# Moving three 8 KB buffers and one odd one by 32 bytes: the stationary operands of the down products at the same address modulo 256 as the moving ones

## The chip, the cores and the metric

The kernel runs on one core of a Trainium2 chip. The metric is the device time of one execution in microseconds (us), the median of the runs shown. Five engines work side by side: TensorE (PE in the profile, with its weight loads as PEld) multiplies, VectorE (DVE) and ScalarE (ACT) do elementwise work, GpSimd (POOL) a little, and SyncE (SP) issues the DMAs that bring the weights from HBM. A matmul has two operands in SBUF: the *stationary* one, which a weight load (LDWEIGHTS) puts into the array, and the *moving* one, whose columns are then streamed through it. SBUF addresses below are bytes within a partition.

## What is computed

One decoder layer on 256 tokens of width 2048, float32 throughout:

```python
x = layer_norm(alpha * x + 0.5 * swiglu(x, ffn1_w_gate, ffn1_w_up, ffn1_w_down), ln1_g, ln1_b)
p = x @ w_in                                   # 2048 x 6432
o_attn = diff_attn_group(p[..., :3072], ...)   # 8 heads, causal, ALiBi, two softmaxes subtracted
o_rwkv = rwkv7_group(p[..., 3072:], ...)       # 16 heads of 64, delta-rule state
x = layer_norm(alpha * x + concatenate([o_attn, o_rwkv], -1) @ w_out, ln2_g, ln2_b)
x = layer_norm(alpha * x + 0.5 * swiglu(x, ffn2_w_gate, ffn2_w_up, ffn2_w_down), ln3_g, ln3_b)

def swiglu(x, w_gate, w_up, w_down):           # D_FF = 5632
    return (jax.nn.silu(x @ w_gate) * (x @ w_up)) @ w_down
```

The nine products with the big weight matrices (gate, up and down of two FFNs, the input projection, the output projection) hold nearly all the arithmetic.

## The kernel before

**Dense products.** Every float32 factor is split into a high part in the fp32r format and the low rest, also fp32r, and a product is three matmuls: high times high (line 105), high activations times low weights (line 106), low activations times high weights (line 107). The activations, transposed so that the contraction lies along the partitions, are stationary (128 x 128); a row block of weights, 128 x 512, is moving. `Stream.block` walks a column block of 512 output columns in steps of two row blocks: one 512 KB DMA into `raw`, `wh` = the cast by ScalarE (line 128), `wl` = the rest by VectorE (line 129), then six matmuls for each of the two token tiles `tt` (tokens 0 to 127 and 128 to 255). Token tile 1 follows token tile 0 by up to four steps (`LAG`), so that the matmuls of the two stand mixed in the program.

**FFN.** The 11 column blocks `j` of 512 hidden columns come in two halves, of 6 and 5. For each `j` the gate and up products run with the transposed input `xh`/`xl` as stationary tiles; then `up_done` multiplies them, transposes the result `h` on TensorE (line 221) and splits it into the high and low tiles `hh` (lines 229 and 230). When a half is done, the four column blocks of the down product run over its hidden columns, with `hh` stationary: 24 row blocks in the first half, 20 in the second. They are called the *down stages* here; there are four, 2112 matmuls in all on 704 pairs of tiles.

**Where the tiles lie.** SBUF is nearly full, and the `hh` tiles live in buffers of the pool `hp` that the mixer between the FFNs uses for other things. Blocks `j` = 0 to 2 have 8,192-byte buffers for both token tiles (tags `J0` to `J2`); blocks 3 to 5 have one 4,096-byte buffer per token tile (`H0` to `H2` for token tile 0, `H3` to `H5` for token tile 1). `H3` is also the mixer's `praw`, 4 x 257 floats, which makes it 4,112 bytes long. A buffer's address follows from the order in which the tags are first used, each rounded up to 32 bytes:

```
buffer  FFN use (tt = token tile)   before: address, mod 256   after: address, mod 256
J0      j = 0, both tt              21536   32                 25664   64
J1      j = 1, both tt              29728   32                 33856   64
J2      j = 2, both tt              37920   32                 42048   64
H0      j = 3, tt 0                 46112   32                 50240   64
H3      j = 3, tt 1                 50208   32                 21536 + 32 = 21568   64
H1      j = 4, tt 0                 54336   64                 54336   64
H4      j = 4, tt 1                 58432   64                 58432   64
H2      j = 5, tt 0                 62528   64                 62528   64
H5      j = 5, tt 1                 66624   64                 66624   64
xh, xl  16 tiles of 2048 bytes      70720 ...  64              the same
wh, wl  7 buffers of 4096 bytes each   115776 ...  64          the same
```

Within a buffer the tiles that a matmul takes lie 512, 2048 or 4096 bytes apart, so each has its buffer's residue. In the kernel before, the odd length of `H3` is what moves the residue from 32 to 64 for all that come after it.

**The order of work** is set by the program's scheduler, which emits one instruction stream per engine with semaphore waits. The mixer's small matmuls run as background generators between the steps of the input projection.

The mixer's uses of the buffers that move are `AR` (J0), `SV` (J1), `qq` (J2), `lw` and `TT` (H0); `praw`, an output tile and `yt` stay in `H3` at residue 32.

Of the kernel before, what the change touches and what calls it, by code (L numbers as in the profile page):

```python
# [10 lines left out]
F32 = mybir.dt.float32  # L11
F32R = mybir.dt.float32r
# [4 lines left out]
P = 128  # L17
D = 2048
S = 256
DFF = 5632  # L20
NB = 512
# [16 lines left out]
def build(tc, A, out):  # L38
# [3 lines left out]
    hp = ctx.enter_context(tc.tile_pool(name="hp", bufs=1))  # L42
# [2 lines left out]
    sp = ctx.enter_context(tc.tile_pool(name="sp", bufs=2))  # L45
    dp = ctx.enter_context(tc.tile_pool(name="dp", bufs=1, space=bass.MemoryType.DRAM))
    pa = ctx.enter_context(tc.tile_pool(name="pa", bufs=3, space=bass.MemoryType.PSUM))

    HT = {"lw": "H0", "T1": "H1", "T2": "H2", "k": "H4"}
    uid = [0]  # L50

    def nm(s):
        uid[0] += 1
        return f"{s}_{uid[0]}"
# [119 lines left out]
    def ln_tail(tt, y, st, gt, bt, last):  # L174
        mv = sp.tile([P, 2], F32, tag="mv", name=nm("mv"))
        V.bn_aggr(out=mv, in_=st)
        ve = sp.tile([P, 1], F32, tag="ve", name=nm("ve"))
        V.tensor_scalar(out=ve, in0=mv[:, 1:2], scalar1=LN_EPS, scalar2=None, op0=ALU.add)
        rs = sp.tile([P, 1], F32, tag="rs", name=nm("rs"))
        G.tensor_tensor(out=rs, in0=ve, in1=neghalf, op=ALU.pow)  # L180
        for q in range(4):
            c = slice(q * NB, (q + 1) * NB)
            yq = y[q]
            V.scalar_tensor_tensor(out=yq, in0=yq, scalar=mv[:, 0:1], in1=gt[:, c], op0=ALU.subtract, op1=ALU.mult)  # L184
            V.scalar_tensor_tensor(out=yq, in0=yq, scalar=rs, in1=bt[:, c], op0=ALU.mult, op1=ALU.add)  # L185
            if last:
                nc.sync.dma_start(out=out[tt * P:(tt + 1) * P, c], in_=yq)
            else:
                transpose_split(yq, tt, q, xT)
                nc.scalar.dma_start(out=xs[tt][:, c], in_=yq)  # L190

    def load_gb(pool, g, b, tg, tb, after=None):
        gt = (hp if tg == "J0" else pool).tile([P, D], F32, tag=tg, name=nm("lng"))
        bt = pool.tile([P, D], F32, tag=tb, name=nm("lnb"))
        if after is not None:
            G.tensor_copy(out=gt[:, 0:1], in_=after)
            G.tensor_copy(out=bt[:, 0:1], in_=after)
        nc.gpsimd.dma_start(out=gt, in_=g.to_broadcast([P, D]))
        nc.gpsimd.dma_start(out=bt, in_=b.to_broadcast([P, D]))
        return gt, bt  # L200

    def ffn(fp, wg, wu, wd, lg, lb, res, last, extra=None):
        y = [fp.tile([P, D], F32, tag=f"y{t}", name=nm("y")) for t in range(2)]
        st = [sp.tile([P, 4, 6], F32, tag=f"st{t}", name=nm("st"), bufs=1) for t in range(2)]
        gb = []
        j0 = 0
        for half, nj in enumerate((6, 5)):
            hT = {}
            sg = {}

            def gate_done(tt, acc):
                s = fp.tile([P, NB], F32, tag="sg", name=nm("sg"), bufs=2)
                SC.activation(out=s, in_=acc, func=AF.Silu)  # L213
                sg[tt] = s

            def up_done(tt, acc, j):
                h = fp.tile([P, NB], F32, tag="h", name=nm("h"), bufs=2)
                V.scalar_tensor_tensor(out=h, in0=sg[tt], scalar=0.5, in1=acc, op0=ALU.mult, op1=ALU.mult)  # L218
                tr = tr_bank[-1]()
                for i in range(4):  # L220
                    T.transpose(tr[:, i, :], h[:, i * P:(i + 1) * P], ident)  # L221
                if j < 3:
                    if tt == 0:
                        hT[j] = hp.tile([P, 4, 4, P], F32R, tag=f"J{j}", name=nm("hh"))
                    hi, lo = hT[j][:, 2 * tt], hT[j][:, 2 * tt + 1]
                else:
                    hl = hp.tile([P, 2, 4, P], F32R, tag=f"H{3 * tt + j - 3}", name=nm("hh"))
                    hi, lo = hl[:, 0], hl[:, 1]
                SC.copy(out=hi, in_=tr)  # L229
                V.tensor_tensor(out=lo, in0=tr, in1=hi.bitcast(F32), op=ALU.subtract)  # L230
                hT[(tt, j)] = (hi, lo)

            for j in range(nj):
                c0 = (j0 + j) * NB
                stream.block(wg, c0, NB, KX, x_lhs, gate_done)
                stream.block(wu, c0, NB, KX, x_lhs, lambda tt, acc, j=j: up_done(tt, acc, j))

            def h_lhs(tt, k, hT=hT):
                hi, lo = hT[(tt, k // 4)]
                return hi[:, k % 4, :], lo[:, k % 4, :]  # L240

            if half == 0 and extra is not None:
                extra(hT[(0, 0)][0][:, 0, 0:1].bitcast(F32))
            if half == 1:
                gb = load_gb(fp, lg, lb, "lng", "lnb", hT[(0, 0)][0][:, 0, 0:1].bitcast(F32))

            def down_done(tt, acc, n, half=half, hT=hT):
                c = slice(n * NB, (n + 1) * NB)
                if half == 0:
                    rc = fp.tile([P, NB], F32, tag="rc", name=nm("rc"), bufs=2)  # L250
                    G.tensor_copy(out=rc[:, 0:1], in_=hT[(0, 0)][0][:, 0, 0:1].bitcast(F32))
                    nc.scalar.dma_start(out=rc, in_=res[tt][:, c])
                    V.scalar_tensor_tensor(out=y[tt][:, c], in0=rc, scalar=ALPHA, in1=acc, op0=ALU.mult, op1=ALU.add)
                else:
                    V.tensor_tensor(out=y[tt][:, c], in0=y[tt][:, c], in1=acc, op=ALU.add)
                    V.bn_stats(out=st[tt][:, n, :], in_=y[tt][:, c])
                    if n == 3:
                        ln_tail(tt, [y[tt][:, i * NB:(i + 1) * NB] for i in range(4)], st[tt], gb[0], gb[1], last)

            for n in range(4):  # L260
                ks = [(j0 * 4 + k, k) for k in range(nj * 4)]
                stream.block(wd, n * NB, NB, ks, h_lhs, lambda tt, acc, n=n, f=down_done: f(tt, acc, n))
            j0 += nj
# [686 lines left out]
```

## Time and profile before

| | |
|---|---|
| runs | 2022.15, 2024.24, 2021.31 us; median 2022.15 us |
| profiled execution | 2021.85 us; span of its instructions 2020.1 us |
| PE busy | 1976.9 us (98%), 9671 matmul records |
| DVE, ACT busy | 1149.0 us (57%), 887.6 us (44%) |
| DMA | 373.35 MB, 185 GB/s on average |
| mean granted TensorE clock | 0.989 |
| first FFN, first half | gate and up to 283.4 us, down stage from there to 406.1 us |
| first FFN, second half | gate and up alone from 417.2 to 627.4 us, down stage alone from 639.2 to 745.4 us |
| mixer, output projection, and gate and up of the second FFN's first half | 746.9 to 1534.2 us |
| second FFN, its two down stages | 1546.0 to 1668.6 us and 1901.8 to 2007.9 us |

Between two stages the matmuls of both stand mixed for about 11 us.

The profile's page gives busy times by engine, the span in 40 slices, and groups of instructions by source line with the tiles that they write and read; windows give the same for a stretch of time. A matmul record's duration includes the time that its data needs through the array, so the records of neighbouring matmuls overlap; the distance from one start to the next is the time that one matmul costs. In a timeline view a row is one instruction or, with "x2", a few merged ones, with its start in microseconds from the span's start.

### The profile page before, as it was taken

To read this page: it belongs to the slowest core of one execution; us is meant where nothing else is said; L and a number is where in the kernel's file an instruction comes from. 1 tells how busy PE (TensorE), PEld (TensorE's weight loads), DVE (VectorE), ACT (ScalarE), POOL (GpSimd) and SP (SyncE) were. 2 spreads that over 40 slices of the span, in tenths; PEclk is the share of its full clock that TensorE was granted. 3 is DMA by queue.
4 is the path that set the end of the run, shared out by engine and by line. 5 is a ranking of instruction groups with operands and counts; after the bars stand their busy time and mean duration, and the time that the engine had idled before them with its cause. 6 is when DMAs were issued, how large, how long until landed. Compare 5 with 4: busy or idle time off the path is not lost. (4 is left out here: it accounts for less than half of the span.)

```text
span 2020.1 us, 24928 instructions
## 1 busy us (share of the span) xinstructions
PE 1976.9 (98%) x9671; PEld 1614.6 (80%) x9671; DVE 1149.0 (57%) x1420; ACT 887.6 (44%) x1100; POOL 33.9 (2%) x68
## 2 busy tenths in 40 slices
PE   9999999999999999999999988999999999999997
PEld 7888888888888878888777777788888888888886
DVE  5555544445554566776677866755554444555455
ACT  5444433344444337645574444444443334444432
POOL 0200000000000000000000000000000000000000
PEclk9999999999999999999999979999999999999999
DMA  7766666667666556556435624666666666766553
GB/s 248 214 188 195 186 190 202 205 192 229 193 187 189 188 171 194 177 160 178 139 86 177 198 84 148 210 198 188 196 185 190 203 204 191 230 193 187 189 188 125
DMA packets 202008, 373.35 MB, mean 185 GB/s; under 512 B 22826, under 2 KB 24944, under 8 KB 201120
## 3 DMA queue, kind: packets, MB, share of 16 engines
q1 hardware_dynamic: 182928, 350.53, 58.0%
q10 hardware_dynamic: 17440, 14.29, 2.4%
q0 software_dynamic: 1520, 6.93, 1.0%
q8 instruction: 76, 1.25, 0.3%
q14 instruction: 44, 0.36, 0.1%
HBM read 364.10 MB, written 7.60 MB: 184 GB/s over the span
## 5 line engine op out<-in xcount | busy, mean ns | idle before, releaser
L129 DVE TENSOR_TENSOR wl<-raw,wh 128x1024 fp32r<-128x1024 f32 (+1 forms) x665 | 808.2, 1216 | 662.4 <-ACT wh L128 661.3
L128 ACT CAST wh<-raw 128x1024 fp32r<-128x1024 f32 (+1 forms) x665 | 695.2, 1046 | 851.9 <-PE acc L107 736.8
L107 PE MATMUL acc<-wh,xl 128*128 128x512 f32 (+1 forms) x1952 | 740.7, 391 | 1.6 <-DVE xl L79 1.6
L106 PE MATMUL acc<-wl,xh 128*128 128x512 f32 (+1 forms) x1952 | 736.7, 392 | 1.0 <-DVE wl L129 1.0
L105 PE MATMUL acc<-wh,xh 128*128 128x512 f32 (+1 forms) x1952 | 725.5, 392 | 9.0 <-ACT xh L78 7.6
L105 PEld LDWEIGHTS acc<-wh,xh 128*128 128x128 f32 x1952 | 367.9, 189 | 88.7 <-ACT xh L78 9.3
L106 PEld LDWEIGHTS acc<-wl,xh 128*128 128x128 f32 x1952 | 368.1, 189 | 77.5 <-issue 2.0
L107 PEld LDWEIGHTS acc<-wh,xl 128*128 128x128 f32 x1952 | 367.8, 188 | 76.3 <-DVE xl L79 2.0
L107 PE MATMUL acc<-wh,hh 128*128 128x512 f32 x704 | 258.0, 395 | 0.0
L106 PE MATMUL acc<-wl,hh 128*128 128x512 f32 x704 | 256.7, 394 | 0.0
L105 PE MATMUL acc<-wh,hh 128*128 128x512 f32 x704 | 256.0, 394 | 0.0
L106 PEld LDWEIGHTS acc<-wl,hh 128*128 128x128 f32 x704 | 132.0, 187 | 31.4
L107 PEld LDWEIGHTS acc<-wh,hh 128*128 128x128 f32 x704 | 132.0, 188 | 31.2
L105 PEld LDWEIGHTS acc<-wh,hh 128*128 128x128 f32 x704 | 132.0, 188 | 30.9
L230 DVE TENSOR_TENSOR hh<-tr,hh 128x512 fp32r<-128x512 f32 x44 | 30.4, 691 | 64.4 <-ACT hh L229 64.4
L229 ACT CAST hh<-tr 128x512 fp32r<-128x512 f32 x44 | 25.8, 586 | 91.7 <-PE tr L221 91.6
L218 DVE SCALAR_TENSOR_TENSOR h<-sg,acc 128x512 f32<-128x512 f32 x44 | 30.3, 688 | 35.6 <-PE acc L107 35.6
L213 ACT ACTIVATE sg<-acc 128x512 f32<-128x512 f32 x44 | 26.4, 600 | 43.8 <-PE acc L107 43.7
L577 DVE TENSOR_TENSOR itmp<-U,Y 64x31 f32<-64x31 f32 (+15 forms) x62 | 20.6, 332 | 11.5 <-DMA U<-dU 10.2
L221 PEld LDWEIGHTS tr<-ident,h 128*128 128x128 f32 x176 | 21.8, 139 | 5.7
L221 PE MATMUL tr<-ident,h 128*128 128x128 f32 x176 | 26.3, 272 | 0.0
L579 DVE TENSOR_TENSOR Y<-Y,itmp 64x31 f32<-64x31 f32 (+15 forms) x62 | 20.6, 332 | 1.4
(247 smaller groups left out, 750.2 us busy)
## 6 DMA issues: line engine op xcount, KB each, us to landing
raw<-in_ffn_w_up_dram SPq DMA_DIRECT2D x176, 512.0 KB, 3.9
raw<-in_ffn_w_down_dram SPq DMA_DIRECT2D x176, 512.0 KB, 4.1
raw<-in_ffn_w_gate_dram SPq DMA_DIRECT2D x175, 512.0 KB, 3.9
raw<-in_w_in_dram SPq DMA_DIRECT2D x96, 512.0 KB, 3.9
raw<-in_w_out_dram SPq DMA_DIRECT2D x32, 512.0 KB, 4.6
rc<-xs ACTq DMA_DIRECT2D x16, 256.0 KB, 4.0
lng<-in_ln_g_dram POOLq DMA_DIRECT2D x3, 1024.0 KB, 7.0
lnb<-in_ln_b_dram POOLq DMA_DIRECT2D x3, 1024.0 KB, 9.3
```

The lines of the kernel that those rows point to most:

```text
L105: T.matmul(a, hi, wh[:, j, :w], start=(ki + j == 0), stop=False)
L106: T.matmul(a, hi, wl[:, j, :w], start=False, stop=False)
L107: T.matmul(a, lo, wh[:, j, :w], start=False, stop=(ki + j == last))
L128: SC.copy(out=wh[:, c, :w], in_=raw[:, c, :w])
L129: V.tensor_tensor(out=wl[:, c, :w], in0=raw[:, c, :w], in1=wh[:, c, :w].bitcast(F32), op=ALU.subtract)
L213: SC.activation(out=s, in_=acc, func=AF.Silu)
L218: V.scalar_tensor_tensor(out=h, in0=sg[tt], scalar=0.5, in1=acc, op0=ALU.mult, op1=ALU.mult)
L221: T.transpose(tr[:, i, :], h[:, i * P:(i + 1) * P], ident)
L229: SC.copy(out=hi, in_=tr)
L230: V.tensor_tensor(out=lo, in0=tr, in1=hi.bitcast(F32), op=ALU.subtract)
L577: V.tensor_tensor(out=tv, in0=U[:, 0:j, j:j + 1].to_broadcast([64, j, 32 - j]), in1=Y[:, j:j + 1, j:32].to_broadcast([64, j, 32 - j]), op= ...
L579: V.tensor_tensor(out=Y[:, 0:j, j:32], in0=Y[:, 0:j, j:32], in1=tv, op=ALU.add)
```

## The change

Two edits. `H3` gets its first use before every other tag of its pool, by a tile that nothing reads or writes, of 4 x 258 floats = 4,128 bytes; so it lies first, at 21536, and the other buffers of the pool follow it at 25664 and on, all at residue 64. And the FFN's use of `H3` starts 8 floats, 32 bytes, into the buffer, at 21568, which is residue 64 too; the tiles of `H0`, `H1`, `H2`, `H4` and `H5` are written in the same flat form without the offset. After it, every stationary and every moving tile of all the dense products lies at 64 modulo 256.

```diff
@@ -45,6 +45,8 @@
     dp = ctx.enter_context(tc.tile_pool(name="dp", bufs=1, space=bass.MemoryType.DRAM))
     pa = ctx.enter_context(tc.tile_pool(name="pa", bufs=3, space=bass.MemoryType.PSUM))
+
+    hp.tile([P, 4 * (S + 2)], F32, tag="H3", name="h3")
 
     HT = {"lw": "H0", "T1": "H1", "T2": "H2", "k": "H4"}
@@ -224,8 +226,10 @@
                     hi, lo = hT[j][:, 2 * tt], hT[j][:, 2 * tt + 1]
                 else:
-                    hl = hp.tile([P, 2, 4, P], F32R, tag=f"H{3 * tt + j - 3}", name=nm("hh"))
-                    hi, lo = hl[:, 0], hl[:, 1]
+                    n = 3 * tt + j - 3
+                    o = 8 if n == 3 else 0
+                    hl = hp.tile([P, o + 8 * P], F32R, tag=f"H{n}", name=nm("hh"))
+                    hi, lo = [hl[:, o + c:o + c + NB].rearrange("p (a b) -> p a b", a=4) for c in (0, NB)]
                 SC.copy(out=hi, in_=tr)
                 V.tensor_tensor(out=lo, in0=tr, in1=hi.bitcast(F32), op=ALU.subtract)
```

No instruction is added, removed or moved: on every engine the two programs have the same instructions in the same order, with the same semaphore waits; only addresses differ.

## The prediction

> **What bounds the kernel now.** The page first: busy time by engine, the slices of the span, the groups that prepare the weights, and two windows, the first down stage and the gate and up products that follow it. (A window's columns: its length, then busy time and instructions of PE, PEld, DVE, ACT and POOL, the granted clock, DMA share, GB/s.)
>
> ```profile
> PE 1976.9 (98%) x9671; PEld 1614.6 (80%) x9671; DVE 1149.0 (57%) x1420; ACT 887.6 (44%) x1100; POOL 33.9 (2%) x68
> PE   9999999999999999999999988999999999999997
> PEclk9999999999999999999999979999999999999999
> ```
>
> ```profile
> L129 DVE TENSOR_TENSOR wl<-raw,wh 128x1024 fp32r<-128x1024 f32 x655 | 800.8, 1224 | 659.3 <-ACT wh L128 658.1
> L128 ACT CAST wh<-raw 128x1024 fp32r<-128x1024 f32 x655 | 688.6, 1052 | 836.7 <-PE acc L107 728.2 <-DMA raw<-in_w_in_dram 44.0 <-DMA raw<-in_ffn_w_gate_dram 22.8
> ```
>
> ```profile
> 283.00:406.00 123.00, 123.00 (x534) 99.56 (x533) 59.48 (x53) 46.71 (x45) 1.10 (x6) 1.00 0.65 200
> 417.00:628.00 211.00, 211.00 (x948) 174.72 (x947) 104.95 (x94) 89.22 (x95) 1.36 (x4) 1.00 0.68 200
> ```
>
> TensorE has work in every slice of the FFNs, at the full granted clock. Inside the two windows it is busy all the time, VectorE about half and ScalarE 38 to 42%, and ScalarE's cast mostly waits for matmuls to free a weight buffer, not the other way round. So the FFN's time is the number of matmuls times the distance between two starts, and anything that changes that distance goes to the end one for one.
>
> Next that distance itself. The first view is a timeline inside a down stage (start, duration, instruction); I matched the 7,968 `acc` records of the trace one by one with the program's matmuls to know which `hh` tile each takes.
>
> ```profile
> 303.36 0.39 PE L105 MATMUL acc<-wh,hh 128*128 128x512 f32 x1
> 303.59 0.39 PE L106 MATMUL acc<-wl,hh 128*128 128x512 f32 x1
> 303.82 0.39 PE L107 MATMUL acc<-wh,hh 128*128 128x512 f32 x1
> 304.04 0.39 PE L105 MATMUL acc<-wh,hh 128*128 128x512 f32 x1
> 304.27 0.39 PE L106 MATMUL acc<-wl,hh 128*128 128x512 f32 x1
> 304.50 0.40 PE L107 MATMUL acc<-wh,hh 128*128 128x512 f32 x1
> 304.73 0.39 PE L105 MATMUL acc<-wh,hh 128*128 128x512 f32 x1
> 304.96 0.40 PE L106 MATMUL acc<-wl,hh 128*128 128x512 f32 x1
> 305.20 0.39 PE L107 MATMUL acc<-wh,hh 128*128 128x512 f32 x1
> 305.43 0.40 PE L105 MATMUL acc<-wh,hh 128*128 128x512 f32 x1
> 305.66 0.39 PE L106 MATMUL acc<-wl,hh 128*128 128x512 f32 x1
> 305.90 0.40 PE L107 MATMUL acc<-wh,hh 128*128 128x512 f32 x1
> 306.13 0.39 PE L105 MATMUL acc<-wh,hh 128*128 128x512 f32 x1
> ```
>
> The first six take tiles at 64 modulo 256, the seven from 304.73 tiles at 32. Starts of the six: (304.50 - 303.36) / 5 = 228 ns apart; of the seven: (306.13 - 304.73) / 6 = 233 ns. Same moving buffers, same stage, no wait in between. Longer stretches sharpen it: from 317.22 on, 48 matmuls in a row have stationary tiles at 32, and the next row at 328.42 is the first at 64; from 417.18 to 454.58 lie 166 matmuls of the gate and up products, whose tiles are all at 64.
>
> ```profile
> 317.22 0.39 PE L105 MATMUL acc<-wh,hh 128*128 128x512 f32 x1
> ...
> 328.42 0.40 PE L105 MATMUL acc<-wh,hh 128*128 128x512 f32 x1
> ```
>
> ```profile
> 417.18 0.39 PE L105 MATMUL acc<-wh,xh 128*128 128x512 f32 x1
> ...
> 454.58 0.39 PE L105 MATMUL acc<-wh,xh 128*128 128x512 f32 x1
> 454.81 0.60 PE L221 MATMUL tr<-ident,h 128*128 128x128 f32 x4
> 455.16 0.47 PE L106 MATMUL acc<-wl,xh 128*128 128x512 f32 x1
> ```
>
> 48 gaps in 11.20 us are 233.3 ns; 165 gaps in 37.40 us are 226.7 ns. The groups by line of stretches inside these two say the same in the records' durations:
>
> ```profile
> L105 PE MATMUL acc<-wh,hh 128*128 128x512 f32 x16 | 5.7, 395 | 0.0
> ```
>
> ```profile
> L105 PE MATMUL acc<-wh,xh 128*128 128x512 f32 x55 | 19.9, 389 | 0.0
> ```
>
> That the place in the block (which `j`) makes the difference, and not the address, is unlikely: `H0` and `H3` have the shape and the neighbours of `H1` and `H4`, and their matmuls go with the slow ones.
>
> **The change part by part.** *The buffers J0 to J2, H0 and the FFN's part of H3 move to 64.* With 4 column blocks, 2 token tiles and 3 matmuls per row block, the first half's down stage has 24 row blocks, of which j = 0 to 3 are 16: 4 x 2 x 16 x 3 = 384 matmuls at 32. The second half has 20 row blocks, again 16 of them: 384. Over two FFNs 1,536 matmuls. At 233.3 - 226.7 = 6.6 ns each that is 10.1 us. Two checks bound it. From above, the stages' own length:
>
> ```profile
> 283.43 0.39 PE L105 MATMUL acc<-wh,hh 128*128 128x512 f32 x1
> ...
> 405.83 0.63 PE L107 MATMUL acc<-wh,hh 128*128 128x512 f32 x2
> ```
>
> ```profile
> 639.20 0.39 PE L105 MATMUL acc<-wh,hh 128*128 128x512 f32 x1
> ...
> 745.36 0.39 PE L107 MATMUL acc<-wh,hh 128*128 128x512 f32 x1
> ```
>
> The first is 122.40 us for 526 gaps and one group of four transposes, which cost 455.16 - 454.58 - 0.23 = 0.35 us. All at 226.7 ns they would take 526 x 0.2267 + 0.35 = 119.6 us: 2.8 us less. The second, 106.16 us for 455 gaps and one such group, would take 103.5 us: 2.7 less. Scaled to the 576 and 480 matmuls of a stage, and twice, this is 2 x (2.8 x 576/526 + 2.7 x 480/455) = 11.8 us, which also counts small stalls that the change does not touch. From below: not every stretch at 64 runs at 226.7; if the down stages came out 0.8 ns slower per matmul than that, 2,112 x 0.8 = 1.7 us would be missing, 8.4 us. I take 10.0.
>
> Nothing takes TensorE's place as the bound there. A step of twelve matmuls will take 12 x 226.7 = 2.72 us, against 1.22 us of VectorE and 1.05 us of ScalarE (rows above), and the gate and up products already run at this pace with the same traffic, 200 GB/s at a DMA share of 0.68.
>
> The Trainium skill has a rule that speaks against the change: "TensorE: Matmul & The Clock Gate", section "Step-by-step: what each phase is for", says that TensorE reads SBUF through two independent ports and that loading the next tile's weights takes nothing from the running matmul's reads. By it the residue could not matter and the sum would be 0; the two stretches above (233.3 against 226.7 ns) contradict it, if the address is what tells them apart.
>
> *The reserved tile* costs no instruction, and 16 bytes. *The offset of 32 bytes and the flat form* leave what ScalarE and VectorE write into `hh` unchanged in shape; lines 229 and 230 run in the shadow of TensorE. I put both at 0.
>
> *The mixer's uses of the moved buffers.* `AR`, `SV`, `qq`, `lw`, `TT` go from 32 to 64. These matmuls are plain float32 and 32 to 256 columns long; their partners lie at 192, 224, 96 or 64 and do not move, so some pairs come nearer and some go apart.
>
> ```profile
> L554 PE MATMUL sm<-AR,BKc 64*128 64x128 f32 x128 | 12.8, 282 | 0.0
> L669 PE MATMUL sm<-Q,SV 128*64 128x64 f32 x128 | 7.9, 245 | 0.0
> L652 PE MATMUL sm<-SV,BT 128*64 128x64 f32 x96 | 6.1, 258 | 3.1 <-DVE SV L645 1.6 <-ACT SV L646 1.5
> L644 PE MATMUL sm<-Rs,TT 64*64 64x64 f32 x128 | 6.1, 240 | 1.1 <-DVE Rs L638 1.1
> ```
>
> These four groups have 480 records, and the others that change about as many again. The trace has no such pair with equal residues, so bounds: the full 6.6 ns on each of some 960 is 6.3 us either way; scaled to 64 of 512 columns it is 0.8 us. The nearest row is the group of transposes at 454.81, float32 too, with residues 128 and 224: 0.60 us for four, of which the last record's length is 0.27, so 0.11 us each, where the gate and up products' pace for four times the columns at half the speed would give 2 x 226.7 / 4 = 0.113. No surplus shows there. I take 0, nearer to the lower bound, and keep 2 us for the range.
>
> *The clock.* TensorE waits in the mixer, and the granted clock falls there:
>
> ```profile
> 1140.00:1200.00 60.00, 49.65 (x540) 40.15 (x539) 41.12 (x118) 27.68 (x77) 4.03 (x4) 0.80 0.36 107
> 1200.00:1350.00 150.00, 140.38 (x651) 114.12 (x650) 95.34 (x115) 61.82 (x69) 3.43 (x6) 0.95 0.60 183
> ```
>
> That is 0.20 x 60 + 0.05 x 150 = 19.5 us of full-speed time in this execution. The change shifts the mixer by 5 us, which may place these stretches differently; the three runs before, whose spread is 2.9 us, are my measure of that: 1.5 us either way.
>
> The sum: 2021.85 - 10.0 = 2011.85 us for an execution like the profiled one. That lies 0.3 us under the median of the runs shown, so the median I forecast is 2022.15 - 10.0, rounded to **2012.2 us**, 0.5% faster.
>
> **The rivals.** *The address has no part in it* (the tiles' place in the block, or their age, sets the pace). For it: every slow tile is also an early one, j = 0 to 3. Against it: the step from 233 to 227 falls exactly between `H0` and `H1` and between `H3` and `H4`, buffers alike in all but their residue. Time: as before, 2022.2 us; 4%.
>
> *Weight loads and moving reads do not disturb each other at all*, and the longer gaps come from something that goes with the early tiles, such as what VectorE and ScalarE do meanwhile. Against it: in the windows above neither engine has more to do per matmul in the down stage than in gate and up: VectorE 59.48 us for 534 records and 104.95 for 948, 0.111 both; ScalarE 46.71 and 89.22, 0.087 and 0.094. Time: 2022.2 us; 2%. This is what the two-port rule of "TensorE: Matmul & The Clock Gate" in the Trainium skill (section named above) would make of the change.
>
> *Only part arrives*, because the mixer's small matmuls take some back: at two thirds of the far bound, 4.2 us, the time would be 2016.4. Against it speaks the transposes' pace. 6%.
>
> *Slower: what decides is the residue modulo 64, and the small matmuls pay far more for it.* Before, `AR`, `SV` and `TT` (32) agree modulo 64 with `BKc` and `Q` (224) and `Rs` and `St` (96); after, at 64, they don't. Those are lines 554, 636, 644, 669 and 675, 304 matmuls of the program on the delta rule's chain. From 10.0 us / 304 = 33 ns each on, it takes the gain; at 45 ns the time is 2022.2 - 10.0 + 13.7 = 2025.9 us. For it: a weight load is a larger share of a short matmul, and windows of the mixer have TensorE waiting, so the chain counts. Against it: the price is five times that of a 512-column matmul. 4%.
>
> *More arrives*: the upper check, 11.8 us, with 1 us from the mixer's pairs: 2009.4 us. Inside the range, 6%.
>
> **How the numbers follow.** The forecast has 78%, the others 4, 2, 6, 4 and 6. The range for 8 in 10: from 2009.2 us (the upper check and the clock's luck) to 2016.5 (the partial case; it also takes in 8.4 us of gain with 2 us lost in the mixer). A difference under 0.2%, 4 us, cannot be told from none. Faster by more: forecast, more, and most of the partial case, 0.89; within: the two cases of no change and a rest, 0.07; slower: 0.04.
>
> **What would show it.** Right: in the groups by line, the `hh` matmuls' mean falls from 394-395 to 389 ns, as with `xh`; 48 matmuls at the head of a down block take 10.9 us, not 11.2; the first two down stages shrink from 122.4 to about 119.7 and from 106.2 to 103.6; gate and up windows are unchanged. Wrong: `hh` still at 394, then the address isn't the cause; `hh` at 389 and the time unmoved, then something after the FFN takes it back, to be seen in the mixer's length between the first and the second FFN, and in lines 554, 644 and 669. Another pace than 226.7, fast or slow, would say that it is not the equality of residues alone that counts.

## The result, and the profile after

| | before | after |
|---|---|---|
| median of 6 runs | 2022.48 us | 2011.24 us |
| lowest to highest | 2021.31 to 2024.92 | 2010.04 to 2018.43 |
| ratio | | 0.9949, 95% interval 0.9934 to 0.9965 |
| span of the profiled execution | 2020.1 us | 2009.6 us |
| mean granted clock in it | 0.989 | 0.991 |

The change makes the kernel 0.5% faster: 11.2 us between the medians, 10.5 between the two traces.

The groups by line of the down products, before and after; the diff's two new lines ahead of them move 105 to 107 down to 107 to 109 (columns: count, busy time in us, mean duration in ns, idle time ahead):

```profile
L107 PE MATMUL acc<-wh,hh 128*128 128x512 f32 x704 | 258.0, 395 | 0.0
L106 PE MATMUL acc<-wl,hh 128*128 128x512 f32 x704 | 256.7, 394 | 0.0
L105 PE MATMUL acc<-wh,hh 128*128 128x512 f32 x704 | 256.0, 394 | 0.0
```

```profile
L109 PE MATMUL acc<-wh,hh 128*128 128x512 f32 x704 | 254.4, 390 | 0.0
L108 PE MATMUL acc<-wl,hh 128*128 128x512 f32 x704 | 253.5, 389 | 0.0
L107 PE MATMUL acc<-wh,hh 128*128 128x512 f32 x704 | 252.7, 389 | 0.0
```

The mean duration falls from 394 to 395 ns to 389 to 390. The same two windows as in the prediction show where the time went: the second, gate and up, is as it was (948 records in 211 us), and the first, a down stage, takes 546 records in 123 us instead of 534.

```profile
283.00:406.00 123.00, 123.00 (x546) 101.88 (x545) 61.05 (x54) 48.03 (x47) 1.11 (x6) 1.00 0.66 205
417.00:628.00 211.00, 211.00 (x948) 174.76 (x947) 104.83 (x94) 89.61 (x95) 1.36 (x4) 1.00 0.68 200
```

The timeline gives the length of the two down stages of the first FFN, between the same matmuls as before:

```profile
285.29 0.39 PE L107 MATMUL acc<-wh,hh 128*128 128x512 f32 x1
...
404.99 0.61 PE L109 MATMUL acc<-wh,hh 128*128 128x512 f32 x2
...
638.15 0.39 PE L107 MATMUL acc<-wh,hh 128*128 128x512 f32 x1
...
741.75 0.39 PE L109 MATMUL acc<-wh,hh 128*128 128x512 f32 x1
```

119.70 us where it was 122.40, and 103.60 where it was 106.16. Following each `acc` matmul by its place in the program, from before to after: from the first to the last `hh` matmul of a down stage, each FFN gains 2.9 us in its first stage and 2.7 us in its second, 11.3 us together (525.6 us before, 514.3 after); the stretch between the FFNs' down stages is 1.4 us shorter; and the start, up to the 200th `acc` matmul, is 2.1 us *longer*. Neither of the last two comes from the addresses. The start's loss is TensorE's clock, seen in the durations of the first matmuls, before and after:

```profile
8.33 0.63 PE L107 MATMUL acc<-wh,xl 128*128 128x512 f32 x1
8.75 0.50 PE L105 MATMUL acc<-wh,xh 128*128 128x512 f32 x1
9.09 0.39 PE L106 MATMUL acc<-wl,xh 128*128 128x512 f32 x1
```

```profile
10.12 0.63 PE L107 MATMUL acc<-wh,xh 128*128 128x512 f32 x1
10.54 1.06 PE L74 MATMUL tr<-ident,xc 128*128 128x128 f32 x4
11.25 0.78 PE L108 MATMUL acc<-wl,xh 128*128 128x512 f32 x1
11.83 0.62 PE L109 MATMUL acc<-wh,xl 128*128 128x512 f32 x1
12.26 0.43 PE L108 MATMUL acc<-wl,xh 128*128 128x512 f32 x1
```

The last matmul of 0.62 to 0.63 us ends at 9.0 us in one execution and at 12.5 in the other; the trace's first record of the full granted clock stands at 9.0 and at 12.3 us. In three further traces of kernels with the same instructions (H3 undone, everything 32 bytes on, and the kernel before once more, all below) the full clock begins between 8.1 and 10.4 us and the 200th matmul comes 0.1 to 0.7 us later than in the first trace, here 2.1 us: one execution differs from another.

The 1.4 us come from the start of the second FFN. In the 34.3 us from its first matmul on, the granted clock is 0.90 before (from 1262.7 us) and 1.00 after (from 1259.6 us). That too differs between executions: it is 0.90 again in the second trace of the kernel before and with everything 32 bytes on, and 0.95 with H3 undone. From this first matmul to the last ahead of the down stage, the three traces at 0.90 take 270.0 to 270.1 us, the one at 0.95 takes 268.6 and the one at 1.00 takes 268.1.

### The profile page after: what moved, and what is told of

Its sections match the earlier page's. It is cut to its first block, busy times and chain, and to the rows that moved or that the text cites. A ratio compares the mean times of both kernels' runs of the same rounds, so it can differ in the third digit from the quotient of the medians.

```text
span 2009.6 us, 24928 instructions
## 1 busy us (share of the span) xinstructions
PE 1964.6 (98%) x9671; PEld 1614.0 (80%) x9671; DVE 1148.2 (57%) x1420; ACT 888.1 (44%) x1100; POOL 34.3 (2%) x68
## 5 line engine op out<-in xcount | busy, mean ns | idle before, releaser
L109 PE MATMUL acc<-wh,hh 128*128 128x512 f32 x704 | 254.4, 390 | 0.0
L107 PE MATMUL acc<-wh,hh 128*128 128x512 f32 x704 | 252.7, 389 | 0.0
L581 DVE TENSOR_TENSOR itmp<-U,Y 64x31 f32<-64x31 f32 (+15 forms) x62 | 20.5, 331 | 11.5 <-DMA U<-dU 10.2
```

Of the source, the lines that this page charges most:

```text
L107: T.matmul(a, hi, wh[:, j, :w], start=(ki + j == 0), stop=False)
L109: T.matmul(a, lo, wh[:, j, :w], start=False, stop=(ki + j == last))
L581: V.tensor_tensor(out=tv, in0=U[:, 0:j, j:j + 1].to_broadcast([64, j, 32 - j]), in1=Y[:, j:j + 1, j:32].to_broadcast([64, j, 32 - j]), op= ...
```

## The experiments

Four theories stood at the outset, all with the observed step from 233 to 227 ns, numbered as in the first expectations: (1) the residues of the two operands' addresses modulo 256 must be *equal*; (2) the stationary tile's own *alignment* to 64 bytes decides; (3) the residues must be equal modulo 64; (4) the *place* of the tile in the block or its age decides and the address is incidental. Below, two operands with equal residues modulo 256 are called *in step*, others *out of step*.

### One part undone: H3 back at 32

```diff
-                    o = 8 if n == 3 else 0
+                    o = 0
```

> The changed kernel without its second edit: the FFN's use of the buffer H3 starts at the buffer's own address, 32 modulo 256, all else at 64. Both theories that blame the address: the 192 matmuls with H3 as stationary tile go back to about 233 ns, 1.3 us in all, and those of J0 to J2 and H0 stay at 226.7; time 2012.5 us. Theory 4 (place in the block, not address): no difference between H3 and the others.

Measured: one run of 2011.05 us, which cannot tell 1.3 us from the scatter of the changed kernel's runs (2010.0 to 2018.4). The trace can. This timeline stretch of the first down stage has six matmuls on tiles at 64 (from 303.07), six on `H3` (from 304.44), and then tiles at 64 again (305.84):

```profile
303.07 0.39 PE L107 MATMUL acc<-wh,hh 128*128 128x512 f32 x1
...
304.44 0.39 PE L107 MATMUL acc<-wh,hh 128*128 128x512 f32 x1
...
305.84 0.40 PE L107 MATMUL acc<-wh,hh 128*128 128x512 f32 x1
```

(304.44 - 303.07) / 6 = 228 ns, (305.84 - 304.44) / 6 = 233 ns. Over the whole trace the 192 matmuls on `H3` come 233.8 ns after the one before on average, those on `J0` to `J2` 226.9. The four down stages take 516.1 us in all against 514.3 in the changed kernel, 1.8 us and not 1.3: matmuls on other tiles right behind one on `H3` are late too, 52 gaps at 231.6 ns. So each of the two edits carries its own share, and the place in the block is out: `H3` is slow with the offset taken away and fast with it, while its neighbours stay fast.

### Everything 32 bytes on: alignment or difference

```diff
+    cp.tile([P, 8], F32, tag="pad", name="pad")
     neghalf = cp.tile([P, 1], F32, tag="neghalf", name="neghalf")
```

> The changed kernel with 32 more bytes reserved ahead of the pool, so that every stationary and every moving tile of the dense products lies at 96 modulo 256 instead of 64. Theory 1 (equal residues): hh and xh matmuls at 389 ns mean and 226.7 ns apart as in the changed kernel, time 2011 us, within 3. Theory 2 (stationary tiles at a multiple of 64 bytes): all 7968 matmuls pay 6.6 ns, 2011 + 52 = 2063 us.

Measured: 2010.89 us; no trace of the 52 us that alignment to 64 bytes would cost. The down products by line:

```profile
L110 PE MATMUL acc<-wh,hh 128*128 128x512 f32 x704 | 254.6, 390 | 0.0
L109 PE MATMUL acc<-wl,hh 128*128 128x512 f32 x704 | 253.5, 389 | 0.0
L108 PE MATMUL acc<-wh,hh 128*128 128x512 f32 x704 | 252.8, 389 | 0.0
```

The four down stages take 514.3 us in all, as in the changed kernel. Both operands at 96 is as good as both at 64. What counts is where one stands relative to the other.

### The other operand moved: the groups change places

On the kernel before, only the weight buffers move, from 64 to 32:

```diff
+    wp.tile([P, 56], F32, tag="pad", name="pad")
     neghalf = cp.tile([P, 1], F32, tag="neghalf", name="neghalf")
```

> The kernel before with 224 bytes reserved ahead of the weight buffers, so that the moving tiles lie at 32 modulo 256 and no stationary tile moves: J0 to J2, H0 and H3 stay at 32, H1, H2, H4, H5 and all xh, xl at 64. If the residues' difference decides, the two groups change places: matmuls on J0 to J2, H0 and H3, slow before, run 226.7 ns apart, those on H1, H2, H4, H5 and the gate and up products about 233. Gate and up of both FFNs: 4224 x 6.6 = 28 us over the changed kernel, the 576 hh matmuls that are now unequal 4 us, the mixer's and output projection's 1632 at 2.5 ns (what the 128-byte experiment showed there) to 6.6 ns 4 to 11 us: 2047 to 2054 us. If the tiles' place in the block or their age decides, J0 to H3 stay at 233 and the others at 227, 2022 us.

Measured: one run of 2045.31 us (the kernel before, run beside it, took 2023.94), a little under the expected band. The slow and the fast group have changed places: gaps on `J0` to `J2`, `H0` and `H3`, whose addresses are those of the kernel before, have a median of 227 ns, and those on `H1`, `H2`, `H4` and `H5` 232 to 233. The two long stretches of the prediction, the 48 matmuls on tiles at 32 and the 166 of gate and up, stand here as

```profile
323.63 0.40 PE L106 MATMUL acc<-wh,hh 128*128 128x512 f32 x1
...
334.53 0.39 PE L106 MATMUL acc<-wh,hh 128*128 128x512 f32 x1
...
423.21 0.40 PE L106 MATMUL acc<-wh,xh 128*128 128x512 f32 x1
...
461.71 0.39 PE L106 MATMUL acc<-wh,xh 128*128 128x512 f32 x1
```

10.90 / 48 = 227 ns where it was 233, and 38.50 / 165 = 233 ns where it was 227. The gate and up products of the first FFN's second half show it in their groups by line, 395 to 397 ns where it was 389:

```profile
L108 PE MATMUL acc<-wh,xl 128*128 128x512 f32 x299 | 113.6, 397 | 0.0
L107 PE MATMUL acc<-wl,xh 128*128 128x512 f32 x299 | 112.1, 397 | 0.0
L106 PE MATMUL acc<-wh,xh 128*128 128x512 f32 x298 | 110.1, 395 | 0.0
```

From start to start the gate and up products average 6.3 ns more than in the changed kernel (912 matmuls with their transposes: 237.1 against 230.8), 26.6 us on 4,224, not 28. The down stages take 521.5 us in all, 7.2 more than in the changed kernel and not 4 (some 0.9 of it on 144 gate and up matmuls that stand mixed in): the tiles in step are mixed with others out of step, the gap needs five to eight matmuls to come down from 234 ns to 227, and so the gaps on tiles at 32 average 228.8. The 1,632 matmuls of the mixer and the output projection take 522.4 us against 517.8, 4.6 us more, at the lower end of 4 to 11. The start was 1.2 us shorter than in the changed kernel's trace. The miss of 2 us is thus spread over several terms, and one run doesn't tell more.

### How far apart may they be

The changed kernel with its weight buffers 128 bytes on, so that the moving tiles lie at 192 and the stationary ones at 64:

```diff
+    wp.tile([P, 32], F32, tag="pad", name="pad")
     neghalf = cp.tile([P, 1], F32, tag="neghalf", name="neghalf")
```

> The changed kernel with 128 bytes reserved ahead of the weight buffers, so that all moving tiles of the dense products lie at 192 modulo 256 and all stationary ones at 64. What counts is the difference modulo 256 (the first table: 232.5 to 233.4 ns at a difference of 128): 7968 matmuls at some 6 ns more, 48 to 53 us, time 2060 us, within 6. Equality modulo 64 or 128 would be enough: 2011 us. Only the FFN's TensorE-bound stages pay and the mixer hides its part (some 1250 of the 7968): 2052 us.

Measured: 2051.12 us median (2050.01 to 2052.45), ratio to the kernel before 1.014, interval 1.0122 to 1.0158. So equal residues modulo 64 or 128 are not enough, and of the expectations the last fits by its number, the one that lets the mixer hide its part. The gate and up products, with their transposes, come 236.6 ns apart against 230.8: 5.9 ns on each.

```profile
L110 PE MATMUL acc<-wh,xl 128*128 128x512 f32 x1920 | 739.9, 397 | 1.1 <-DVE xl L82 1.1
L109 PE MATMUL acc<-wl,xh 128*128 128x512 f32 x1920 | 736.5, 398 | 0.7 <-DVE wl L132 0.7
L108 PE MATMUL acc<-wh,xh 128*128 128x512 f32 x1920 | 723.9, 397 | 7.7 <-ACT xh L81 7.3 <-ACT wh L131 0.2
L110 PE MATMUL acc<-wh,hh 128*128 128x512 f32 x704 | 258.7, 396 | 0.0
```

The 1,632 matmuls of the mixer and the output projection take 523.1 us here; in the five traces whose residues are equal in this stretch (the kernel before twice, the changed one, H3 undone, everything 32 bytes on) they take 516.9 to 517.8. That is 5.2 to 6.2 us, where 5.9 ns each would be 9.6: the mixer hides a third to a half of its part, not the whole. That it is hidden where TensorE waits for other things is likely and was not traced.

### The disputed cost by itself

A kernel of nothing but groups of 48 matmuls, each group in two passes; its core is

```python
        for i in range(REP):
            k, m = i % 8, (i // 2) % 2
            T.matmul(acc[:, :cols], stf[:, so + k * P:so + (k + 1) * P], mvf[:, mo + m * NB:mo + m * NB + cols],
                     start=(i == 0), stop=(i == REP - 1))
```

`REP` is 48, `stf` and `mvf` are the stationary and the moving tile, and `so` and `mo` their shifts in elements.

> This kernel leaves out the whole layer: it copies the first 128 tokens into a stationary tile and a moving tile (float32r) that both start at 64 modulo 256, and runs groups of 48 matmuls of 128x512, eight stationary slots 512 bytes apart in turn. Group statA has both operands at 64; statB to statQ shift the stationary slots by 16 bytes more each, up to 256; moveA to moveQ shift the moving operand instead; bothA to bothO shift both. fullA, C, E, I are plain float32 and halfA, C, E, I bfloat16, with the stationary operand 0, 32, 64 and 128 bytes on. Theory 1 (equal residues modulo 256): 226.7 ns from start to start in statA, statQ, moveA, moveQ and every both group, about 233 ns in all others. Theory 2 (the stationary tile must start at a multiple of 64 bytes): statA, E, I, M, Q at 226.7, all move groups at 226.7, bothC and bothG at 233. Theory 3 (equal residues modulo 64): statA, E, I, M, Q and moveA, E, I, M, Q and every both group at 226.7, the others at 233. Theory 4 (the address has no part in it): all at 226.7. For plain float32 and bfloat16 no theory has a row; if the mixer's unchanged matmuls tell, plain float32 shows no difference.

The groups by line (96 matmuls in two passes; the gap from start to start is (busy / 2 - mean) / 47, so 22.1 us is 227 ns and 22.7 us is 233; plain float32 has two records to a matmul, and two of the 96 bfloat16 records are missing):

```profile
L50 PE MATMUL fullA<-raw 128*128 128x512 f32 x192 | 82.7, 592 | 0.0
L50 PE MATMUL fullC<-raw 128*128 128x512 f32 x192 | 82.7, 592 | 0.0
...
L50 PE MATMUL moveC<-mv,st 128*128 128x512 f32 x96 | 22.7, 395 | 0.0
L50 PE MATMUL statI<-mv,st 128*128 128x512 f32 x96 | 22.7, 395 | 0.0
L50 PE MATMUL statE<-mv,st 128*128 128x512 f32 x96 | 22.7, 396 | 0.0
L50 PE MATMUL statC<-mv,st 128*128 128x512 f32 x96 | 22.7, 395 | 0.0
...
L50 PE MATMUL bothC<-mv,st 128*128 128x512 f32 x96 | 22.2, 390 | 0.0
L50 PE MATMUL bothG<-mv,st 128*128 128x512 f32 x96 | 22.2, 390 | 0.0
...
L50 PE MATMUL statQ<-mv,st 128*128 128x512 f32 x96 | 22.1, 389 | 0.0
...
L50 PE MATMUL halfA<-mvb,stb 128*128 128x512 bf16 x94 | 20.9, 379 | 0.1
L50 PE MATMUL halfC<-mvb,stb 128*128 128x512 bf16 x94 | 20.9, 379 | 0.1
```

At a shift of 256 (statQ) the pair is as good as in place, at 32, 64 and 128 (C, E, I) it is not, and shifting both (bothC, bothG) does no harm. Plain float32 and bfloat16 do not care, at the shifts of 0, 32, 64 and 128 bytes that were tried. All mean gaps, in ns, from the trace's start times:

```
bytes   stationary on   moving on        bytes   stationary on   moving on
0       229.1 (*)       226.7            144     233.4           233.3
16      226.7           231.6            160     233.3           234.2
32      233.2           233.4            176     229.9           233.3
48      233.3           233.2            192     228.9           233.2
64      233.2           229.1            208     233.3           234.5
80      231.8           231.0            224     233.4           233.4
96      234.2           233.6            240     227.1           226.8
112     233.3           231.2            256     226.7           227.5
128     233.4           232.5            both on 226.7 to 227.2 at all eight shifts
(*) 226.7 in the first pass; the second begins with a gap of 418 ns and settles at 227 after ten matmuls
```

Theory 1, equal residues modulo 256, tells the fast groups for every shift that is a multiple of 32, the step in which the allocator places buffers. The price is not the same for all: the stationary operand 192 on, or the moving one 64 on, which is the same difference, costs only 2.2 to 2.4 ns instead of 6.6. Four groups 16 bytes from equal do not follow it: three run at 227, one (moving 16 on) at 231.6.

The note under the table is a finding too: with equal residues the stream falls into a state, and it takes some matmuls to get there. In statA's second pass the gaps after the first are 229, 234, 235, 225, 230, 236, 229, 232, 231 and then 227 for the rest. Group bothC, 32 bytes on with both operands, follows bothA, which ran at 227, and its gaps still begin with 230, 223, 232, 235, 229, 232 and 231. With the stationary operand 128 on the gaps alternate, 229 and 238, to the end of the group.

### Finer shifts, fewer columns

The same kernel with shifts of 4 bytes, and with fewer moving or stationary columns:

> Leaves out the whole layer, as the first table does: groups of 48 float32r matmuls of 128x512, stationary slots and moving tile at 64 modulo 256. statA to statQ shift the stationary slots by 4 bytes more each, 0 to 64; moveA to moveQ the moving operand. oneEq/oneOff, twoEq/twoOff, threeEq/threeOff have 128, 256, 384 moving columns, narrow, mid, broad 32, 64, 96 stationary columns, each with the stationary operand in place (Eq) and 32 bytes on (Off). Theory 1, a stall in the running matmul for each line of the stationary tile that the next load reads, more of them when the two streams are out of step: in place 512 columns and 10 to 11 ns of stall (226.7 against 216 for bfloat16), Off some 17 ns; the stall grows with the stationary columns (a quarter, a half, three quarters of it at 32, 64, 96) and does not depend on the number of moving columns, so 163.3, 109.9, 56.6 plus 10 and plus 17 ns at 384, 256, 128. Theory 2, the moving stream itself is slower per column out of step: the surplus of Off over Eq is 6.6 ns times the share of moving columns, and the same for any number of stationary columns. Shifts below 16 bytes: theory 1 with 16-byte lines says 226.7 up to 16 (the first table has 226.7 at +16), then 233.

```profile
L50 PE MATMUL narrowOff<-mv,st 128*32 128x512 f32 x96 | 23.3, 402 | 0.0
...
L50 PE MATMUL narrowEq<-mv,st 128*32 128x512 f32 x96 | 22.5, 394 | 0.0
...
L50 PE MATMUL broadEq<-mv,st 128*96 128x512 f32 x96 | 22.4, 392 | 0.0
L50 PE MATMUL broadOff<-mv,st 128*96 128x512 f32 x96 | 22.3, 390 | 0.0
L50 PE MATMUL statA<-mv,st 128*128 128x512 f32 x96 | 22.1, 390 | 0.0
L50 PE MATMUL threeEq<-mv,st 128*128 128x384 f32 x96 | 17.0, 334 | 0.0
L50 PE MATMUL threeOff<-mv,st 128*128 128x384 f32 x96 | 17.0, 336 | 0.0
L50 PE MATMUL twoEq<-mv,st 128*128 128x256 f32 x96 | 11.9, 284 | 0.0
L50 PE MATMUL twoOff<-mv,st 128*128 128x256 f32 x96 | 11.7, 281 | 0.0
```

Both theories of the mechanism fall. Of theory 1's times in place, 173.3 and 119.9 ns at 384 and 256 moving columns come out (173.4 and 120.8), but 66.6 at 128 does not (110.6), and its surplus out of step is not there. A quarter of the stationary columns does not give a quarter of the stall: with 32 columns the gap is 231.4 ns in place and 239.4 with 32 bytes between, with 64 it is 230.0 and 231.6, with 96 it is 230.0 and 228.9. Three quarters of the moving columns show no surplus at all: 173.4 and 173.3 ns; at 256 columns the shifted group is even 2.5 ns faster (118.3 against 120.8), at 128 columns 1.1 ns slower (111.7 against 110.6). So the rule of equal residues is shown for 128 stationary and 512 moving columns of float32r, and for these sizes alone; with others another difference may be the good one, or none. Of the 4-byte shifts from 4 to 64 none reaches the pace of equal residues (the best is 228.4). And the stationary operand 16 bytes on, at 226.7 ns in the first table, runs at 233.4 here, where it follows a group out of step instead of one in step: a sign again of a state that depends on what went before. The moving operand 16 bytes on does not show it: 231.6 ns in both kernels.

### The kernel before, once more

> The kernel before once more, for a second trace of it: the down stages at 122.6 and 106.2 us again within 0.1, since no theory has a reason for them to move; the start and the mixer, where the granted clock decides, within 2 us of the first trace. If the mixer's stretch differs by over 1.4 us between the two, its shortening by 1.4 us in the changed kernel says nothing.

Measured: 2022.40 us. Its first down stage begins at 283.52 and its 528th matmul starts at 406.15, 122.63 us as in the first trace, and the second takes 106.15. The stretch from the first matmul after the FFN to the last gate and up matmul ahead of the second FFN's down stage, 787.3 us in the first trace, is 787.8 here, 786.0 in the changed kernel. The two traces of before differ by 0.5 us, so by the expectation the shortening is not their scatter; but it is the clock, as said under the result. The 1,632 matmuls of the mixer and the output projection alone take 517.4 and 517.8 us in the two traces of before, and 517.8, 517.2 and 516.9 in the changed kernel and its two variants with nearly all residues equal. The mixer's matmuls, whose buffers moved by 32 bytes, neither gain nor lose anything that these traces show.

## Why the prediction was right, point by point

**What bounds the kernel.** TensorE's start-to-start distance in the down stages went to the end one for one, as the first step said: nothing took its place at 226.7 ns, and the window of the down stage now has VectorE at 61.05 and ScalarE at 48.03 of 123 us.

**The price per matmul.** 226.7 ns for all tiles, as read from the gate and up stretch. The stages came out at 119.70 and 103.60 us; the prediction had about 119.7 and 103.6. The 48 matmuls at the head of a down block, from 318.40 to 329.28 us in the changed kernel, take 10.88 us; the prediction had 10.9.

**The count and the sum.** The forecast was 2012.2 us, measured are 2011.24. The mis-sized term is the down stages' gain: 10.1 us, taken as 10.0, where the four down stages gave 11.3, nearer to the upper check of 11.8 that I had discounted as containing "small stalls that the change does not touch". The price on the matmuls at 32 was right: their gaps fell from 233.7 to 227.0 ns on average, 10.2 us. What the sum left out are matmuls at 64. One that follows a matmul at 32 was late too, 231 ns: 185 such gaps, 156 of them in the down products, cost 0.8 us, and they are at 227 now. The other gaps at 64 in the down products, 227.2 ns before and 226.6 after, gave 0.2 us. The tables say why: the stream needs some matmuls to fall into step, so a mixed order loses it at each change of residue.

**The clock.** The start cost 2.1 us in the profiled execution, a place that the prediction did not count (it had the clock in the mixer only, 1.5 us either way), and the 1.4 us gained at the second FFN's start are the clock's as well. So it is luck that the two traces differ by 10.5 us, close to the forecast 10.0: 11.3 + 1.4 - 2.1 = 10.6. The medians differ by 11.2.

**The mixer at 0.** Borne out within what three traces against two can tell. That plain float32 matmuls show no surplus was argued from one row of transposes. The trace had nearer rows: line 720's matmuls of 256 columns have both tiles at 224 modulo 256, and their records average 379 ns, as do those of lines 461 and 699, out of step (32 against 192, and 224 against 192). The table has the same for 512 columns, 592 ns and 82.7 us in place and at 32 bytes alike. The rival in which the mixer's short matmuls pay for the residue modulo 64, up to 13.7 us, is refuted by the mixer's own length, 517.8 us where it was 517.4 to 517.8.

**The rivals.** Place or age of the tiles: refuted twice, by `H3` alone and by the exchange of the two groups. The rule of "TensorE: Matmul & The Clock Gate" in the Trainium skill, section "Step-by-step: what each phase is for", that a weight load takes nothing from the running matmul's reads: for bfloat16 and plain float32 the tables agree with it as far as addresses go (20.9 and 82.7 us at the four shifts tried); for float32r the address of the stationary tile changes the pace of the matmuls, 22.1 against 22.7 us a group, so there the measurement decides against it.

**What stays open** is the mechanism. The runs show that the difference of the two addresses matters, with period 256 on the points tried, that what went before has a part in the pace, and that the effect depends on both column counts; what in the two reads collides is not shown.

## What to carry to other kernels

Where a stream of float32r matmuls of 128 stationary and 512 moving columns bounds a kernel, look at the built program's addresses: an odd-sized buffer in a pool can put all later ones out of step with the weights, and bringing every stationary and moving tile to one residue modulo 256 costs a reordered allocation and a few bytes. The stake was 6.6 ns of 233 per matmul: 11 us here, where a fifth of the dense matmuls were out of step, and 40 us (2051.1 against 2011.2) with all of them 128 bytes apart. To find it, compare start-to-start distances between groups of matmuls that differ in nothing but the tile they read; for other sizes measure anew, since at 256 and 384 moving columns a shift of 32 bytes cost nothing.

## What was unexpected of the hardware

- float32r with equal residues runs at 226.7 ns for 512 columns where bfloat16 has 216 (median of the halfA group), and at 173.4 for 384 columns; the 128 columns between them cost 0.416 ns each, which would make 213.2 ns for 512, so by this estimate some 13 ns a matmul do not depend on the columns. No shift tried at 512 columns removed them: the lowest mean is 226.7.
- The good state can be entered and left: a group with equal residues took ten matmuls to reach 227 ns, and a group with the stationary operand 16 bytes on stayed at 226.7 after a group in step, and at 233.4 after one out of step.
- The start of TensorE's full clock moved by 3 us from one execution to another (records at 9.0 and 12.3 us), which cost 2 us of the profiled difference, and a stretch of 34.3 us at a granted clock of 0.90 came in one and not in the other.
